# An MLP up projection in seven products (Strassen) instead of eight, with the down projection as a stage of its own

## The chip, the cores and the metric

The kernel runs on one core of a Trainium2 chip. The metric is device time in microseconds (us) of one execution. The time before is the median of three runs: 3092.51 us (3089.76 to 3093.38).

## The reference, cut to what matters

One decoder layer over 2048 positions of width 1024: a mixer of two attention groups with an output projection, and then a gated MLP. The change concerns the MLP and the place where it begins:

```python
x = x + _rmsnorm(mix, attn_post_norm[l])
h = _rmsnorm(x, ffn_pre_norm[l])                       # 2048 x 1024
u = _causal_depthwise_conv(h @ w_up[l], conv_w[l], conv_b[l])   # w_up: 1024 x 5632, three taps
gate, val = jnp.split(u, 2, axis=-1)                   # 2816 columns each
y = (jax.nn.gelu(gate, approximate=True) * val) @ w_down[l]     # w_down: 2816 x 1024
x = x + _rmsnorm(y, ffn_post_norm[l])
```

## The kernel before

All data are float32. Every operand of a product is split into a part `hi`, copied to the type fp32r, and the rest `lo`, and each product is three matmuls: hi·hi, hi·lo, lo·hi. The helper `split` (L455) makes the two parts: `hi` is a copy on ACT or DVE, `lo` a subtraction on POOL or DVE.

The order of the whole program is made when it is built. Every piece of work is an `op` with an engine, a guessed duration, the ops it depends on, its buffers and a due time (`plan.now` minus `lead`). `Plan.run` (L180) plays a list schedule: at each instant each engine takes the ready op with the earliest due time whose buffers are free, and the instruction is written into that engine's stream. An op with `.alt` goes to whichever of two engines is free first. In the guesses a POOL op and a DVE op never hold each other up (`c_pool(512)` is 1223 ns, `c_dvs(512)` 664 ns), and all transfers, which go through SP's one queue, share 250 GB/s; SP hands out no more than 3 us of transfers ahead. On the chip each engine runs its stream in that fixed order and waits on semaphores. Buffers come from tags with a fixed number of copies, handed out in the order in which the program asked for them.

The output projection runs in blocks of 128 positions (`wo_block`, 16 of them): a load of the mixer's output, 48 matmuls, the post norm, the residual row block `x1` (stored to `x1d`, L1125), the pre norm of the MLP, eight transposes, and a store of the transposed rows to `h2d` (L1148).

The MLP goes over four token tiles of 512 positions (`t`), one after the other. For each tile there are 44 up jobs (22 feature tiles `m` of 128 columns, gate and value, `up`): 8 k-blocks of 128 times three matmuls 128x128 by 512, into one PSUM bank; then DVE and ACT do the convolution's three taps (L1238 to L1240), GELU (L1243) and the product (L1248), and ACT and POOL split the result into `gt` (L1249, L1250), which stays in SBUF. Then come 22 down jobs (`down`, L1311): eight accumulators of 128x512, 24 matmuls for each `m`. Weights are loaded and split for every token tile (`weights`, four jobs ahead). The memory of the MLP's inputs and weights lies where the attention's buffers were (`ffn_left`), so up jobs of tile 0 start before the last output-projection blocks are done; the rest (`ffn_right`) opens when those blocks are.

## Time and profile before

| | |
|---|---|
| median of three runs | 3092.51 us |
| profiled execution | 3094.23 us, of which the span from the first to the last instruction is 3092.5 us |
| TensorE (PE) busy | 2984.5 us, 97% of the span |
| VectorE (DVE) busy | 2252.0 us, 73% |
| ScalarE (ACT), GpSimd (POOL) busy | 1442.9 us (47%), 951.6 us (31%) |
| transfers | 437.11 MB, mean 141 GB/s |
| mean granted TensorE clock | 0.992 |

PE overlaps successive matmuls, so its busy time counts a matmul longer than the distance between two of them. DMA share is the mean busy share of the 16 DMA engines.

### The profile page before, as it was taken

Reading aid. Unit: us, or ns where it says so; the run is one execution under the profiler, and the core shown is the slowest. Engines: PE = TensorE matmul, PEld = TensorE weight load, DVE = VectorE, ACT = ScalarE, POOL = GpSimd, SP = SyncE. Lnnn points to the kernel's source line nnn. Section 1 sums busy time; section 2 is a strip of 40 time slices with the busy share of each in tenths; the row PEclk is TensorE's granted clock in tenths of the full one; section 3 lists DMA queues with packets and bytes.
Section 4 is the critical chain, followed back from the end, with each engine's and each line's share of the span. In section 5 each row is a group of like instructions: output and inputs, shape, how many; then the busy total and the mean of one; then the engine's idle time right before and its main releaser. Section 6 shows DMA issues by size and latency. Waiting matters only on the chain. (4 is left out here: it accounts for less than half of the span.)

```text
span 3092.5 us, 48117 instructions
## 1 busy us (share of the span) xinstructions
PE 2984.5 (97%) x17352; PEld 2610.4 (84%) x17352; DVE 2252.0 (73%) x4327; ACT 1442.9 (47%) x2913; POOL 951.6 (31%) x1047
## 2 busy tenths in 40 slices
PE   7999999999999999889999999999999999999998
PEld 7899999999888888868877888888888888888887
DVE  4658878897999999998754864387744776277742
ACT  4434545555777767666643433233322433233321
POOL 1001002002766777675411211033301332023310
PEclk9999999999999999999999999999999999999999
DMA  8776656655634366533363333443344333343332
GB/s 264 246 209 186 185 151 201 171 156 159 188 122 130 95 194 185 151 100 112 110 214 126 102 100 116 121 134 96 96 129 143 96 99 106 119 141 101 96 123 82
DMA packets 392146, 437.11 MB, mean 141 GB/s; under 512 B 20096, under 2 KB 328164, under 8 KB 381668
## 3 DMA queue, kind: packets, MB, share of 16 engines
q1 hardware_dynamic: 391908, 434.05, 46.7%
q8 instruction: 136, 2.23, 0.3%
q14 instruction: 102, 0.84, 0.1%
HBM read 333.30 MB, written 100.67 MB: 140 GB/s over the span
## 5 line engine op out<-in xcount | busy, mean ns | idle before, releaser
L1226 PE MATMUL pu<-fh,fhi 128*128 128x512 f32 x2816 | 869.0, 390 | 0.2 <-ACT fu L1234 0.2
L1226 PEld LDWEIGHTS pu<-fh,fhi 128*128 128x128 f32 x2816 | 529.4, 188 | 110.5 <-ACT fu L1234 0.6
L461 DVE TENSOR_TENSOR flo<-fraw,fhi 128x1024 fp32r<-128x1024 f32 x186 | 233.0, 1254 | 488.6 <-ACT fhi L458 488.5
L1226 PE MATMUL pu<-fh,flo 128*128 128x512 f32 x1408 | 549.2, 390 | 0.0
L982 POOL TENSOR_TENSOR ring_w<-ring_w,ring_a 128x512 f32<-128x512 f32 (+2 forms) x320 | 387.9, 1224 | 220.3 <-DVE ring_a L977 121.1
L605 PE MATMUL g<-hT,big 128*128 128x256 f32 x3072 | 447.8, 288 | 7.3 <-DVE st L638 4.3
L458 ACT CAST fhi<-fraw 128x1024 fp32r<-128x1024 f32 x253 | 265.5, 1051 | 397.4 <-PE py L1311 218.6
L1311 PE MATMUL py<-fhi,gt 128*128 128x512 f32 x1408 | 435.9, 390 | 0.0
L605 PEld LDWEIGHTS g<-hT,big 128*128 128x128 f32 x3072 | 405.4, 192 | 19.8 <-DVE st L638 4.4
L977 DVE TENSOR_TENSOR_SCAN ring_a<-ring_a 128x513 f32<-128x513 f32 (+2 forms) x320 | 412.8, 1316 | 6.1 <-ACT ring_a L969 6.1
L702 PE MATMUL z<-k,q 128*128 128x512 f32 (+3 forms) x1280 | 362.5, 376 | 10.4 <-ACT ring_a L969 7.0
L466 ACT CAST thi<-t 128x512 fp32r<-128x512 f32 (+2 forms) x472 | 221.6, 492 | 210.1 <-PE t L720 179.3
L1311 PEld LDWEIGHTS py<-fhi,gt 128*128 128x128 f32 x1408 | 264.5, 188 | 60.0
L1226 PEld LDWEIGHTS pu<-fh,flo 128*128 128x128 f32 x1408 | 264.7, 188 | 54.9
L734 DVE TENSOR_TENSOR tlo<-t,thi 128x512 fp32r<-128x512 f32 (+2 forms) x528 | 281.6, 556 | 34.6 <-ACT thi L466 28.4
L459 POOL TENSOR_TENSOR flo<-fraw,fhi 128x1024 fp32r<-128x1024 f32 x78 | 195.8, 2510 | 338.9 <-DVE fhi L457 171.2
L1311 PE MATMUL py<-flo,gt 128*128 128x512 f32 x704 | 277.8, 395 | 0.0
L720 PE MATMUL t<-ident,ring_w 128*128 128x128 f32 x1632 | 253.2, 276 | 22.4 <-DVE tlo L734 18.5
L1250 POOL TENSOR_TENSOR gt<-fy,gt 128x512 fp32r<-128x512 f32 x88 | 118.4, 1347 | 493.9 <-ACT gt L1249 483.0
L1239 DVE SCALAR_TENSOR_TENSOR fy<-fu,cw,fy 128x512 f32<-128x512 f32 x176 | 239.6, 1361 | 6.2
L384 POOL TENSOR_TENSOR sm<-sm,neghalf 128x2 f32<-128x2 f32 (+1 forms) x72 | 76.8, 1067 | 536.5 <-DVE sm L382 534.7
L602 PE MATMUL g<-big,hT 128*128 128x256 f32 x1536 | 227.4, 288 | 6.3 <-DVE st L624 1.5
(158 smaller groups left out, 4697.4 us busy)
## 6 DMA issues: line engine op xcount, KB each, us to landing
fraw<-in_w_up_dram SPq DMA_DIRECT2D x176, 512.0 KB, 3.8
hT<-hd SPq DMA_DIRECT2D x64, 1024.0 KB, 7.0
fraw<-in_w_down_dram SPq DMA_DIRECT2D x88, 512.0 KB, 3.8
q<-qd SPq DMA_DIRECT2D x128, 256.0 KB, 4.3
hd<-hT SPq DMA_DIRECT2D x16, 1024.0 KB, 5.4
qd<-st SPq DMA_DIRECT2D x128, 128.0 KB, 2.6
kd<-st SPq DMA_DIRECT2D x128, 128.0 KB, 2.6
vd<-st SPq DMA_DIRECT2D x64, 256.0 KB, 5.2
```

The lines of the kernel that those rows point to most:

```text
L458: "ACT", c_act(n) + 42, lambda: nc.scalar.copy(hi(), raw()))
L461: "DVE", c_dvs(n), lambda: nc.vector.tensor_tensor(lo(), raw(), f32(hi()), ALU.subtract))
L602: nc.tensor.matmul(ps.t[:, cs], hk[:, b, c * P:(c + 1) * P], wv[:, a, k, :], start=first, stop=last)
L605: nc.tensor.matmul(ps.t[:, cs], wv[:, a, k, c * P:(c + 1) * P], hk[:, b, :], start=first, stop=last)
L702: nc.tensor.matmul(ps.t[:, 0:w], q.t[:, m, l, jj * P:(jj + 1) * P], kt.t[:, m, 0:w], start=(l == 0), stop=(l == 1 and not masked))
L720: nc.tensor.transpose(ps.t[:, cc * P:(cc + 1) * P], rows[jj].t[:, (k + kk) * P:(k + kk + 1) * P], ident)
L734: ol = op("DVE", c_dvp(n), lambda sl=sl: nc.vector.tensor_tensor(lo.t[:, sl], ps.t[:, sl], f32(hi.t[:, sl]), ALU.subtract), (oh,), (ps, hi ...
L977: nc.vector.tensor_tensor_scan(gr, gr, gr, 1.0 if cb is None else cb[0].t[:, 0:1], ALU.mult, ALU.bypass)
L982: rdeps.append(op("POOL", c_pool(w), lambda be=be, gm=gm, w=w: nc.gpsimd.tensor_tensor(be.t, be.t, gm.t[:, 1:w + 1], ALU.mult), (o1, o2), ...
L1226: nc.tensor.matmul(ps.t, w3(w)[:, k, :], h.t[:, a, k, :], start=(k == 0 and i == 0), stop=(k == KD - 1 and i == 2))
L1239: nc.vector.scalar_tensor_tensor(y.t, u.t[:, 1:TT + 1], cw[:, 1, f:f + 1], y.t, ALU.mult, ALU.add)
L1311: nc.tensor.matmul(ps.t, gt.t[:, a, j * P:(j + 1) * P], wt.t[:, ms], start=(m == 0 and i == 0), stop=(m == NFT - 1 and i == 2))
```

## The change

The up projection of gate and value over two token tiles of 512 is seen as a product of two 2x2 block matrices: rows gate and value by two halves of K (weights), two halves of K by two token tiles (inputs). The Winograd form of Strassen's scheme needs seven block products instead of eight, with sums of blocks on both sides and sums of the products after. `S` is a pair of token tiles, so there are 44 up steps (`S`, `m`) with 7 times 12 matmuls each.

`combos` builds the seven input blocks, split, one k-block at a time, from `h2q` and stores them in DRAM (`bd`); `load_b` loads the seven of a pair (2 MB each), five into memory that opens with `ffn_left` and two into `ffn_right`. `up_weights` loads four weight quarters, makes four sums on DVE and seven splits. `up` runs the seven products, copies the first from PSUM, makes seven sums of PSUM and SBUF tiles on DVE, and convolves both tiles at once (1024 wide; the first tap on ACT). The gated product is split and stored to `gtd`. The down projection is a loop of its own: for each (`t`, `m`) it loads and splits 2 x 256 KB of weights and loads 512 KB of `gtd`. The order is up of pair 0, down of tile 0, up of pair 1, down of tiles 1 to 3. `ffn_left` opens at the attention's end as before, but everything that an up step needs besides the input blocks now lies in `ffn_right`.

```diff
-    h2d = [dram.tile([P, KD, P], F32, name=f"h2d{i}") for i in range(NB)]
+    h2q = [dram.tile([P, KD, TT], F32, name=f"h2q{t}") for t in range(NTT)]
+    bd = [dram.tile([P, 2 * 4 * TT], F32, name=f"bd{i}") for i in range(14)]
+    gtd = [dram.tile([NFT, P, 2 * TT], F32, name=f"gtd{t}") for t in range(NTT)]
...
-                h2d[b].rearrange("p k n -> p (k n)"), h2.t), ops, (h2,), 0, 1 << 19, "h2store")
+                h2q[b // 4][:, :, b % 4 * P:(b % 4 + 1) * P], h2.t.rearrange("p (k n) -> p k n", k=KD)), ops, (h2,), 0, 1 << 19, "h2store")
...
-    for name, n in (("fraw", 2), ("fhi", 4), ("flo", 4), ("fh", 1), ("fu", 2), ("fy0", 2), ("fy1", 2), ("yh", 4),
-                    ("x1", 1), ("o1", 2), ("junk", 1), ("gt", NFT), ("pu", 4), ("py", 4), ("fs", 16)):
-        T[name] = Tag(n, fifo=name != "fs", bank=name in ("pu", "py"))
...
+    PROD = ("11", "21", "t2", "t1", "t3", "22", "t4")
+    for name, n in (("hb", 4), ("gt", 3), ("B", 5), ("B2", 2), ("Wc", 7), ("wr", 5), ("sS", 2), ("sa", 4), ("fu", 2),
+                    ("y", 2), ("fs", 16), ("pf", 8)):
+        T[name] = Tag(n, fifo=name != "fs", bank=name == "pf")
...
+        fill_tags(hp, {"hb": ([P, 512], F32), "gt": ([P, 2, TT], F32R), "B": ([P, 2, 4, TT], F32R)})
...
+        fill_tags(gp, {"B2": ([P, 2, 4, TT], F32R), "Wc": ([P, 2, 512], F32R), "wr": ([P, 512], F32),
+                       "sS": ([P, 512], F32), "sa": ([P, 512], F32), "fu": ([P, 2 * TT + 2], F32),
+                       "y": ([P, 2 * TT], F32), "fs": ([P, 4], F32)})
+        fill_tags(pool(rpsum, "pf8", "right", PSUM), {"pf": ([P, 512], F32)})
...
+    def combos(S, k):
+
+        def get(half, t):
+            b = buf("hb")
+            tt = 2 * S + t
+            return b, load(lambda: b.t, h2q[tt][:, half * 4 + k, :], 1 << 18, (b,),
+                           [h2store[4 * tt + j] for j in range(4)], what="hbload")
+
+        def sub(x, y):
+            (a, ao), (b, bo) = x, y
+            d = buf("hb")
+            return d, op("DVE", c_dvs(512), lambda: nc.vector.tensor_tensor(d.t, a.t, b.t, ALU.subtract), (ao, bo),
+                         (d, a, b), what="hsub")
+
+        def emit(name, x):
+            a, ao = x
+            g = buf("gt")
+            o = split(lambda: a.t, lambda: g.t[:, 0, :], lambda: g.t[:, 1, :], 512, (ao,), (a, g), 0.0)
+            bstore[S, name].append(op(SPE, 0, lambda: nc.sync.dma_start(
+                bd[S * NC7 + PROD.index(name)].rearrange("p (a k n) -> p a k n", a=2, k=4)[:, :, k, :], f32(g.t)), o,
+                (g,), 0, 1 << 19, "bstore"))
+
+        b11, b12 = get(0, 0), get(0, 1)
+        t1 = sub(b12, b11)
+        emit("11", b11)
+        b22 = get(1, 1)
+        t3 = sub(b22, b12)
+        emit("t1", t1)
+        t2 = sub(b22, t1)
+        emit("22", b22)
+        emit("t3", t3)
+        b21 = get(1, 0)
+        t4 = sub(b21, t2)
+        emit("t2", t2)
+        emit("21", b21)
+        emit("t4", t4)
...
+    def load_b(S):
+        for i, name in enumerate(PROD):
+            b = buf("B" if i < 5 else "B2")
+            assert len(bstore[S, name]) == 4
+            btile[S, i] = b, load(lambda b=b: f32(b.t).rearrange("p a k n -> p (a k n)"), bd[S * NC7 + i], 1 << 21, (b,),
+                                  bstore[S, name], lead=10e3, what="bload")
...
+    def up_weights(S, m):
+        raw = {}
+        for i, c in ((0, 0), (0, 1), (1, 0), (1, 1)):
+            r = buf("wr")
+            f = i * NFT + m
+            raw[i, c] = r, load(lambda r=r: r.t.rearrange("p (k n) -> p k n", k=4),
+                                up_src[:, c * 4:(c + 1) * 4, f * P:(f + 1) * P], 1 << 18, (r,), lead=0.0, what="wup")
+
+        def comb(d, x, y, alu, deps=()):
+            (a, ao), (b, bo) = x, y
+            return d, op("DVE", c_dvs(512), lambda: nc.vector.tensor_tensor(d.t, a.t, b.t, alu), (ao, bo, *deps),
+                         (d, a, b), what="wsub")
+
+        res = []
+
+        def emit(x):
+            a, ao = x
+            w = buf("Wc")
+            res.append((w, split(lambda: a.t, lambda: w.t[:, 0, :], lambda: w.t[:, 1, :], 512, (ao,), (a, w), 0.0)))
+
+        emit(raw[0, 0])
+        emit(raw[0, 1])
+        s1 = comb(buf("sS"), raw[1, 0], raw[1, 1], ALU.add)
+        s2 = comb(buf("sS"), s1, raw[0, 0], ALU.subtract)
+        emit(s2)
+        emit(s1)
+        emit(comb(buf("sS"), raw[0, 0], raw[1, 0], ALU.subtract))
+        emit(comb(s2[0], raw[0, 1], s2, ALU.subtract, res[2][1]))
+        emit(raw[1, 1])
+        return res
...
+    def up(S, m):
+        ws = made.pop(("U", S, m))
+
+        def prod(i):
+            ps, (w, wd), (b, bl) = buf("pf"), ws[i], btile[S, i]
+            o = None
+            for k2 in range(2):
                 def go(k2=k2):
+                    wv = w.t.rearrange("p a (k n) -> p a k n", k=4)
                     for k in (2 * k2, 2 * k2 + 1):
-                        for i, (w, a) in enumerate(((hi, 0), (hi, 1), (lo, 0))):
-                            nc.tensor.matmul(ps.t, w3(w)[:, k, :], h.t[:, a, k, :],
-                                             start=(k == 0 and i == 0), stop=(k == KD - 1 and i == 2))
-                last = op("PE", 6 * c_mm(512), go, [*ls, *wd, last] if last else [*ls, *wd], (hi, lo, h, ps), what="up")
-                plan.now += 6 * c_mm(512)
+                        for n, (x, y) in enumerate(((0, 0), (0, 1), (1, 0))):
+                            nc.tensor.matmul(ps.t, wv[:, x, k, :], b.t[:, y, k, :], start=k == 0 and n == 0,
+                                             stop=k == 3 and n == 2)
+                o = op("PE", 6 * c_m2(512), go, [*wd, bl] + ([o] if o else []), (ps, w, b), what="up")
+            plan.now += 12 * c_m2(512)
+            return ps, o
...
+        p1 = prod(0)
+        a = buf("sa")
+        a = a, copy(lambda a=a: a.t, lambda: p1[0].t, 512, (p1[1],), (p1[0], a))
+        c11 = add(ua(fg), fg, a, prod(1))
+        b = part(a, prod(2))
+        p5 = prod(3)
+        d = part(b, p5)
+        c = part(b, prod(4))
+        c22 = add(ub(fv), fv, c, p5)
+        c12 = add(ub(fg), fg, d, prod(5))
+        c21 = add(ua(fv), fv, c, prod(6))
...
+            o = op("ACT", c_act(2 * TT) + 95, lambda: nc.scalar.activation(
+                y.t, u.t[:, 0:2 * TT], AF.Identity, scale=sc(0), bias=sc(3)), (o0, *deps, *mem["cw"]), (u, y),
+                what="conv")
+            for i in (1, 2):
+                o = op("DVE", c_dvs(2 * TT), lambda i=i: nc.vector.scalar_tensor_tensor(
+                    y.t, u.t[:, i:2 * TT + i], sc(i), y.t, ALU.mult, ALU.add), (o,), (u, y), what="conv")
...
+        for t in range(2):
+            sl = slice(t * TT, (t + 1) * TT)
+            g = buf("gt")
+            o1 = op("DVE", c_dvs(512), lambda sl=sl: nc.vector.tensor_tensor(yv.t[:, sl], yg.t[:, sl], yv.t[:, sl],
+                                                                           ALU.mult), (o, og), (yg, yv))
+            os_ = split(lambda sl=sl: yv.t[:, sl], lambda g=g: g.t[:, 0, :], lambda g=g: g.t[:, 1, :], 512, (o1,),
+                        (yv, g), 0.0)
+            gstore[2 * S + t, m] = op(SPE, 0, lambda g=g, t=t: nc.sync.dma_start(
+                gtd[2 * S + t][m], f32(g.t).rearrange("p a n -> p (a n)")), os_, (g,), 0, 1 << 19, "gstore")
...
+    def down_weights(t, m):
+        ws = []
+        for h in range(2):
+            r, w = buf("wr"), buf("Wc")
+            o = load(lambda r=r: r.t, w_down[0, m * P:(m + 1) * P, h * 512:(h + 1) * 512], 1 << 18, (r,), lead=0.0,
+                     what="wdn")
+            ws.append((w, split(lambda r=r: r.t, lambda w=w: w.t[:, 0, :], lambda w=w: w.t[:, 1, :], 512, (o,), (r, w),
+                                0.0)))
+        g = buf("gt")
+        gl = load(lambda: f32(g.t).rearrange("p a n -> p (a n)"), gtd[t][m], 1 << 19, (g,), (gstore[t, m],), lead=0.0,
+                  what="gload")
+        return ws, g, gl
...
+        ss, o, x1 = T["fs"].buf(), buf("y"), buf("fu")
...
+        items = [("U", 0, m) for m in range(NFT)] + [("D", 0, m) for m in range(NFT)] + [
+            ("U", 1, m) for m in range(NFT)] + [("D", t, m) for t in range(1, NTT) for m in range(NFT)]
+        ready = 0
+
+        def prepare(n):
+            nonlocal ready
+            while ready <= min(n, len(items) - 1):
+                kind, a, m = it = items[ready]
+                made[it] = up_weights(a, m) if kind == "U" else down_weights(a, m)
+                ready += 1
+        for n, (kind, a, m) in enumerate(items):
...
+            prepare(n + (1 if kind == "U" and items[min(n + 1, len(items) - 1)][0] == "U" else 3))
+            if kind == "U":
+                up(a, m)
+                if a == 0 and m in (3, 7, 11, 15):
+                    combos(1, (3, 7, 11, 15).index(m))
+            elif m < NFT - 2:
+                down(a, m, range(4))
+                if a == 0 and m == 0:
+                    load_b(1)
+            elif m == NFT - 1:
                 for j in range(4):
-                    for i in range(4):
-                        down(W[n - 1 + i // 2], t, NFT - 4 + i, v, (j,))
+                    for mm in (NFT - 2, NFT - 1):
+                        down(a, mm, (j,))
...
+    op(None, 0, ffn_left, users("k", "v", "q", "thi", "tlo", "mo", "ot", "os", "sq", "mix", "sm", "z", "o", "w", "a"))
     for b in range(8, NB):
         run(wo_block(b))
+        if b < 12:
+            combos(0, b - 8)
+    load_b(0)
```

The parts left out: pools' names, the loaders and helper calls inside the functions shown, the halo copies (as before, two values for each feature tile), GELU and product (as before, 1024 wide and in two halves of 512), `finish` (as the old `half`, 1024 wide, one store of 512 KB), and the removed bodies, which stand in the listing above.

## Rows read from the trace of the kernel before

**Rows 1.** Chain that ended last, in time: start, us, engine, line, matmuls.

```profile
1680.78 12.29 PE pu L1226 x54
...
2002.97 239.36 PE pu L1226 x1056
2242.33 120.86 PE py L1311 x528
```

**Rows 2.** Window, up jobs of tile 1: length, busy PE, PEld, DVE, ACT, POOL (instructions), PEclk, DMA share, GB/s.

```profile
2003.00:2242.00 239.00, 239.00 (x1056) 198.05 (x1055) 181.54 (x266) 90.19 (x131) 83.69 (x45) 1.00 0.38 113
```

**Rows 3.** Groups by line, PE, 1583 to 1682: count, busy us, mean ns.

```profile
L1226 PE MATMUL pu<-fh,fhi 128*128 128x512 f32 x120 | 38.0, 398 | 0.0
```

**Rows 4.** Groups by line, DVE and POOL, up jobs of tile 1 (2003 to 2242).

```profile
L1239 DVE SCALAR_TENSOR_TENSOR fy<-fu,cw,fy 128x512 f32<-128x512 f32 x42 | 65.9, 1568 | 1.5
L1240 DVE SCALAR_TENSOR_TENSOR fy<-fu,cw,fy 128x512 f32<-128x512 f32 x42 | 31.6, 752 | 1.5
L1238 DVE TENSOR_SCALAR fy<-fu,cw 128x512 f32<-128x512 f32 x42 | 31.3, 745 | 0.0
L461 DVE TENSOR_TENSOR flo<-fraw,fhi 128x1024 fp32r<-128x1024 f32 x22 | 28.1, 1276 | 53.9 <-ACT fhi L458 53.9
L1282 DVE TENSOR_TENSOR o<-py,gfpost 128x512 f32<-128x512 f32 x2 | 1.4, 685 | 0.0
L459 POOL TENSOR_TENSOR flo<-fraw,fhi 128x1024 fp32r<-128x1024 f32 x22 | 55.1, 2507 | 47.7 <-ACT fhi L458 44.1 <-DVE fs L1284 3.6
L1250 POOL TENSOR_TENSOR gt<-fy,gt 128x512 fp32r<-128x512 f32 x21 | 27.2, 1298 | 109.7 <-ACT gt L1249 104.2 <-PE pu L1226 5.5
```

**Rows 5.** Instructions in time, DVE and POOL, one conv: start, us.

```profile
2101.64 0.54 DVE L1238 TENSOR_SCALAR fy<-fu,cw 128x512 f32<-128x512 f32 x1
2102.22 2.77 DVE L1239 SCALAR_TENSOR_TENSOR fy<-fu,cw,fy 128x512 f32<-128x512 f32 x1
2105.02 0.75 DVE L1240 SCALAR_TENSOR_TENSOR fy<-fu,cw,fy 128x512 f32<-128x512 f32 x1
2105.69 0.16 DVE L1235 COPY halo<-fu 128x2 f32<-128x2 f32 x1
...
2101.90 2.54 POOL L459 TENSOR_TENSOR flo<-fraw,fhi 128x1024 fp32r<-128x1024 f32 x1 [2.08 <-ACT fhi L458]
```

**Rows 6.** Instructions in time: DVE reading PSUM (`t`) beside POOL, in the attention.

```profile
899.31 1.26 DVE L734 TENSOR_TENSOR tlo<-t,thi 128x512 fp32r<-128x512 f32 x2
...
898.38 1.89 POOL L982 TENSOR_TENSOR ring_w<-ring_w,ring_a 128x512 f32<-128x512 f32 x1 [1.22 <-DVE ring_a L977]
```

**Rows 7.** Groups by line, ACT, 1680 to the end.

```profile
L458 ACT CAST fhi<-fraw 128x1024 fp32r<-128x1024 f32 x244 | 256.1, 1051 | 390.2 <-PE py L1311 218.6 <-PE pu L1226 116.6 <-DMA fraw<-in_w_down_dram 51.9
L1234 ACT COPY fu<-pu 128x512 f32<-128x512 f32 x169 | 98.1, 580 | 9.7 <-DVE fy L1240 5.2 <-DVE halo L1235 4.5
```

**Rows 8.** Windows with the DMA engines full: the last two columns.

```profile
120.00:130.00 10.00, 10.00 (x88) 10.00 (x87) 8.83 (x31) 8.09 (x22) 1.39 (x2) 1.00 0.96 327
510.00:520.00 10.00, 10.00 (x80) 9.64 (x79) 9.37 (x32) 3.98 (x8) 0.00 (x0) 1.00 1.02 291
```

**Rows 9.** DMA issues in time, SP queue, output projection: `x1` of blocks 8, 10, 15.

```profile
1548.47 0.46 SPq L377 DMA_DIRECT2D fraw<-h2d  x1
1550.82 0.33 SPq L1125 DMA_DIRECT2D x1d<-r  x1
...
1583.55 0.33 SPq L1125 DMA_DIRECT2D x1d<-r  x1
...
1685.30 0.33 SPq L1125 DMA_DIRECT2D x1d<-r  x1
```

**Rows 10.** DMA issues by kind: count, KB each, median us to landing.

```profile
fraw<-in_w_up_dram SPq DMA_DIRECT2D x176, 512.0 KB, 3.8
```

**Rows 11.** Instructions in time: the last matmul and the last DVE instruction.

```profile
3083.22 0.39 PE L1311 MATMUL py<-fhi,gt 128*128 128x512 f32 x1
...
3088.72 0.75 DVE L1294 SCALAR_TENSOR_TENSOR o<-o,fs,fh 128x512 f32<-128x512 f32 x1
```

More of the change, by code (lines that the diff above doesn't have):

```diff
@@ new lines, in prod, with add, part @@
+            plan.now += 12 * c_m2(512)
+            return ps, o
+        def add(dst, dbuf, x, p):
+            (a, ao), (ps, o) = x, p
+            return op("DVE", c_dvp(512), lambda: nc.vector.tensor_tensor(dst(), ps.t, a.t, ALU.add), (ao, o),
+                      (ps, a, dbuf), what="uadd")
+        def part(x, p):
+            d = buf("sa")
+            return d, add(lambda: d.t, d, x, p)
+        fg, fv = buf("fu"), buf("fu")
+        ua = lambda f: (lambda: f.t[:, 2:TT + 2])
+        ub = lambda f: (lambda: f.t[:, TT + 2:2 * TT + 2])
@@ L1320, in ffn_all @@
-        AHEAD = 4
-        for j in range(4):
-            load_h2(0, j, ())
-        for n in range(AHEAD):
-            weights(n)
-        for n, (kind, t, m, v) in enumerate(jobs):
-            if n + AHEAD < len(jobs):
-                weights(n + AHEAD)
-            if kind == "up":
-                up(n, t, m, v)
-            elif m < NFT - 4:
-                w = W.pop(n)
-                down(w, t, m, v, range(4))
-                down(w, t, m + 1, v, range(4))
-                if v == 0 and t + 1 < NTT and m in (4, 8, 12, 16):
-                    load_h2(t + 1, m // 4 - 1, (lasts[t, 0, 3],))
-            elif m == NFT - 2:
+            if S == 0:
+                halod[f] = op("DVE", 70, lambda: nc.vector.tensor_copy(halo[:, f, :], u.t[:, 2 * TT:2 * TT + 2]),
+                              (o0, *deps), (u,))
@@ new lines, in layer_kernel, with down, go @@
+    dn = {}
+    def down(t, m, js):
+        ws, g, gl = made["D", t, m]
+        for j in js:
+            for h, (w, wd) in enumerate(ws):
+                if m == 0:
+                    dn[t, j, h] = buf("pf"), None
+                ps, prev = dn[t, j, h]
+                def go(j=j, ps=ps, w=w):
+                    for i, (a, b) in enumerate(((0, 0), (0, 1), (1, 0))):
+                        nc.tensor.matmul(ps.t, g.t[:, a, j * P:(j + 1) * P], w.t[:, b, :],
+                                         start=(m == 0 and i == 0), stop=(m == NFT - 1 and i == 2))
+                dn[t, j, h] = ps, op("PE", 3 * c_m2(512), go, [gl, *wd] + ([prev] if prev else []), (ps, g, w),
+                                     what="dn")
+                plan.now += 3 * c_m2(512)
+            if m == NFT - 1:
+                finish(t, j)
```

168 lines of the change are left out of this document (38 added, 130 removed).

## The prediction

> **What bounds the kernel now.** I read the chain of work that ended last first, because it tells which engine sets the end. Its long last links are TensorE alone: the 1056 matmuls of a token tile's up jobs take 239.36 us and the 528 of its down jobs 120.86 us, one behind the other [rows 1]. That is 0.2267 us for an up matmul and 0.2289 us for a down matmul. Then I read the window of one tile's up jobs: PE full, DVE busy 181.5 of 239 us, POOL 83.7 [rows 2]. So a matmul less is worth its 0.2267 us, as long as nobody makes TensorE wait. The groups of instructions [rows 3, 4, 7], the instructions in time [rows 5, 6], full DMA windows [rows 8] and the SP queue [rows 9, 10] are for what the change puts beside it.
>
> **The terms.** The sum starts from the profiled execution, 3094.2 us (its span and 1.7 us around it); the median of the runs is 1.7 us below.
>
> *Matmuls.* 44 steps of 84 instead of 96: 528 x 0.2267 = 119.7 us less. The 2112 down matmuls stay, and a step of the up projection is now 84 x 0.2267 = 19.0 us, one of the down projection 24 x 0.2289 = 5.5 us. Minus 119.7.
>
> *The beginning of the MLP.* Today up jobs of tile 0 fill the gaps of the last output-projection blocks: 120 hi matmuls and half as many with lo weights between 1583 and 1682 [rows 3], 180 or 40.8 us that are done when, from about 1682 on, up matmuls have PE to themselves [rows 1]. After the change no up matmul can run before `ffn_right` opens, which waits for the last block. So the 40.8 us come back, and the first product starts late. How late: the memory of `ffn_left` is open from 1548 [rows 9]. From there on these transfers stand before the first step: blocks 9 to 15 (7 x 2.1 MB), `combos(0)` (28 stores of 0.52 MB, 16 loads of 0.26 MB), seven tiles of 2.1 MB, the gain and the first weights (1.5 MB); together 49.8 MB. With full DMA engines windows moved 327 and 291 GB/s [rows 8]: 152 to 171 us, middle 162, so 1710. The weights are behind the last two tiles in the queue (these are due 10 us earlier), and behind them come some 2 us to the landing (3.8 for a load of 1.6 us of data [rows 10]) and a split (0.6 + 1.3 [rows 4, 7]): first product at 1714, 32 us after 1682. Term 40.8 + 32 = plus 73. From below: the blocks' own chain. `x1` of block 8 leaves at 1550.8, of block 10 at 1583.6 [rows 9], 16.4 us a block; block 15 would be at 1665, and some 8 us of norm and transposes, a store, 5.7 MB and the split make 1691: plus 50. From above: 20.4 us a block as from 10 to 15 [rows 9], and one tile in the way: 1733, plus 92.
>
> *The tiles of pair 1.* They take the memory that the last step of pair 0 frees. Down steps 0 to 2 are prepared at the beginning of that step, but step 3's loads are due at the beginning of down step 0, and `load_b(1)` is due 4.6 us before that. So in the queue: 3.1 MB of steps 0 to 2, 14.7 MB of tiles, two stores of the gated product, 1.0 MB for step 3. By 327 GB/s the 19.9 MB take 61 us, and 2 us to land; TensorE has work for 19.0 + 3 x 5.5 = 35.5 us. Plus 27 of stall (22 if the two stores stand behind, 35 by 291 GB/s). Down steps later take 1.05 MB per 5.5 us, 191 GB/s, which fits, so nothing is won back. The Trainium skill (HBM Reference, Specifications) says that a core that streams alone measures about 425 GB/s; no window of this trace shows more than 327 (small packets among them). By that rate this stall would be 14 us and the sum 13 us less, an estimate from that page.
>
> *DVE and POOL in an up step.* What DVE gets, in distances between starts (0.67 for two SBUF operands of 512 [rows 5], 0.63 from PSUM [rows 6], some 1.2 for 1024 [rows 4], less the overlap of two): four weight sums 2.7, four taps of 1024 4.8, two products 1.3, seven sums from PSUM 4.4, halo copies 0.3. Of the splits' subtractions the schedule gave DVE 22 and POOL 22 in tile 1, where either could have them [rows 4]; of nine I give DVE 3.5 (2.3 us) and POOL 5.5 (7.1 us by 1.30 [rows 4]). Most `hi` parts go to ACT, which has 2 x 1.05 (first taps), about 1.05 (GELU), 0.6 and 8 x 0.6 = 8.6 us [rows 7] of 19, so they cost nothing; one on DVE 0.35. DVE's sum is 16.2 of 19.0 us. By these durations TensorE still sets the pace, and the term is zero.
>
> But the two engines do not run side by side. In [rows 5] the second tap, two SBUF operands, starts 0.3 us after a POOL subtraction and lasts 2.77 us instead of 0.75: it ends 0.55 us after POOL's end. Over the tile the second tap means 1568 ns against 752 for the same work at the third, and the first tap 745 against 540: 34 + 9 = 43 us that DVE stood, 51% of POOL's 83.7 us [rows 2, 4, 5]. An operation that reads PSUM was not held: two of 0.63 us pass beside a POOL operation [rows 6]. The Trainium skill (SBUF — State Buffer, Who interferes with whom) gives the rule: DVE with two SBUF inputs and GpSimd reading SBUF shut each other out for a whole instruction; the 2.77 us agree. By durations alone the sum would be 3089, with the lock it is that of the next lines.
>
> In the new step DVE has little idle time beside which POOL could pass (before, 57 of 239 us [rows 2]), only the 4.4 us of PSUM sums. So the share of POOL's time that stops DVE lies between 0.51 and, with the PSUM sums as the only cover, 0.78; I take 0.63. A step is 16.2 + 0.63 x 7.1 = 20.6 us, 1.6 over TensorE: 35 us in each pair. Pair 0 also has `combos(1)`: 16 sums and 28 subtractions, 10.7 + 9.4 on DVE, 14 x 1.3 x 0.63 = 11.5 of standing: 32 us more. Of the 102 us I take off 12, since the weights are split one step ahead and the backlog at a pair's end falls into down steps, where DVE is free. Plus 90; from below 28 (share 0.51, all lead used), from above 170 (6.5 subtractions on POOL, 0.78).
>
> *Changes of stage.* The three `gt` copies go to down steps 0 to 2 before the last up step's two, so in pair 1 step 3's load waits for step 2's end: 4 us. In `finish` a third row block waits for the first one's store (two copies of its buffers), and its PSUM banks with it: some 3 us at two tile changes, 2 us elsewhere. Plus 12 (3 to 20). At the end, 10.6 us today from the last matmul [rows 11] to the end of the execution, the same wait adds 3 (1 to 6). The other additions (2.1 MB stores of `h2q`, `gtd`) lie in up steps whose DMA share is 0.38 [rows 2] and stay hidden.
>
> Sum: 3094.2 - 119.7 + 73 + 27 + 90 + 12 + 3 = 3179.5, against the median's base 3178.
>
> **Rivals.** *TensorE keeps the pace in the up steps* (the other side). The place is the up step. POOL's subtractions pass beside sums from PSUM and DVE's remaining gaps; it decides at 2.9 us of standing per step (19.0 - 16.2), a share of 0.41. For it speaks that in tile 1 PE stood nowhere while DVE was busy 76% [rows 1, 2]; against it that half of POOL's time stopped DVE even then. Time: 3179.5 - 90 = 3089, between 3050 and 3128 with the beginning's bounds (50 to 92) and the others': faster where the beginning comes out under 71. Chance 0.24: 0.14 faster, 0.04 equal, 0.06 slower.
>
> *The last block is caught behind the tiles.* Its residual row is due 5 us before the stage's end, the tiles 10 us; if five tiles (10.5 MB) are in the queue before it, `ffn_right` opens 32 us later: 3210. For it: the order of due times; against it, that at 16.4 us a block the row is asked for at about 1660, by when `combos` has hardly let the first tiles go. Chance 0.12.
>
> *The tiles of pair 1 are hidden*, if step 3's loads find a free copy early and pass the tiles: 3151. Against it stands the due time. Chance 0.06.
>
> The forecast itself, DVE and POOL over TensorE in the up steps, has 0.58, with 3105 to 3255 as its own range. About 0.2% (6 us) is what a measurement can tell. Faster: 0.14 of the first rival and 0.04 of the forecast's low end, 0.18; equal 0.06; slower 0.76. The range 3070 to 3262 leaves out the fast half of the first rival and the top of the forecast.
>
> **What would show it.** In the profile after: 3696 up matmuls; a gap of PE of some 30 us or more before the first one, at about 1714; one of some 27 us after the third down step of tile 0; in the up steps PE waiting for `Wc` subtractions, DVE busy 95% or more, taps of 1024 that mean well over 1.3 us, POOL's subtractions over 1.3, pair 0 slower than pair 1 by some 1.4 us a step. Wrong it would be above all if a step of pair 1 takes 19.0 us, or if the first product starts before 1690.

## The result and the profile after

The changed kernel takes 3192.72 us (median of 4 runs, 3190.27 to 3195.74) against 3091.14 us for the kernel before (4 runs): ratio 1.0329, 95% interval [1.0311, 1.0347]. It is slower by 3.3%, in spite of 528 matmuls less. The profiled execution took 3194.84 us, its span 3193.1.

The page of the changed kernel, engine totals and the two costliest groups (their last field is the time that TensorE stood before them):

```profile
PE 2935.2 (92%) x16824; PEld 2531.8 (79%) x16824; DVE 2457.2 (77%) x4479; ACT 1470.9 (46%) x3014; POOL 1122.0 (35%) x1154
...
L1277 PE MATMUL pf<-B,Wc 128*128 128x512 f32 x3696 | 877.2, 399 | 64.0 <-POOL Wc L461 22.9
...
L1364 PE MATMUL pf<-Wc,gt 128*128 128x512 f32 x2112 | 502.1, 400 | 35.7 <-DMA gt<-gtd 33.2
```

Some 100 us of standing lie in the MLP, where before the long links of the chain had none [rows 1]. Windows by stage tell where (the same columns as in [rows 2]): the last output-projection blocks, the wait for the first product, up steps of pair 0, down steps of tile 0, up steps of pair 1, down steps of tiles 1 to 3.

```profile
1547.00:1687.00 140.00, 90.83 (x346) 69.91 (x345) 63.96 (x107) 49.06 (x128) 20.69 (x25) 0.80 0.87 305
1687.00:1725.90 38.90, 8.13 (x37) 6.11 (x35) 5.42 (x13) 7.98 (x25) 1.10 (x2) 0.66 0.59 204
1725.90:2204.80 478.90, 447.38 (x1849) 356.46 (x1850) 460.69 (x587) 188.37 (x270) 248.21 (x141) 0.96 0.41 137
2204.60:2358.90 154.30, 128.85 (x530) 103.15 (x529) 51.90 (x76) 37.53 (x65) 7.45 (x7) 0.90 0.72 259
2358.70:2799.10 440.40, 429.85 (x1849) 346.22 (x1847) 419.21 (x516) 175.27 (x248) 213.62 (x123) 1.00 0.32 106
2801.60:3182.60 381.00, 373.22 (x1584) 299.74 (x1584) 130.27 (x189) 96.27 (x175) 22.80 (x22) 0.99 0.63 209
```

The reader is to see three things: DMA at 305 GB/s ahead of the first product; DVE busy 96% and 95% of the two up stages, with TensorE short of full; and the first down stage 33 us longer than the 120.86 of [rows 1]. TensorE in time, at these three places (the bracket is the idle time before the instruction and what ended it):

```profile
1701.97 1.97 PE L1141 MATMUL t<-ident,r 128*128 128x128 f32 x8 [6.63 <-DVE r L1132]
1725.89 4.47 PE L1277 MATMUL pf<-B,Wc 128*128 128x512 f32 x10 [21.95 <-ACT Wc L460]
...
2219.08 14.09 PE L1364 MATMUL pf<-Wc,gt 128*128 128x512 f32 x48 [7.29 <-DMA gt<-gtd]
2250.16 10.19 PE L1364 MATMUL pf<-Wc,gt 128*128 128x512 f32 x32 [16.99 <-DMA gt<-gtd]
...
2573.30 39.21 PE L1277 MATMUL pf<-B,Wc 128*128 128x512 f32 x168 [1.32 <-POOL Wc L461]
2614.35 26.01 PE L1277 MATMUL pf<-B,Wc 128*128 128x512 f32 x111 [1.84 <-POOL Wc L461]
```

The last two rows show the pace of pair 1 late in the stage: 168 matmuls, two steps, and then 1.84 us of waiting for a GpSimd subtraction. Pair 1 cut at the place where these waits begin:

```profile
2358.70:2572.00 213.30, 213.28 (x921) 172.49 (x919) 203.19 (x253) 85.13 (x122) 102.17 (x60) 1.00 0.33 108
2572.00:2799.00 227.00, 216.47 (x928) 173.73 (x928) 215.92 (x264) 90.14 (x127) 111.42 (x64) 1.00 0.31 105
```

Eleven steps (921 matmuls) run without a gap at 213.3 / 10.96 = 19.5 us each; the next eleven take 227.0 / 11.05 = 20.5. The lock that sets these 20.5 is seen in DVE and POOL in time: at 2576 a DVE subtraction starts 0.2 us after one of POOL and takes 1.64 us, and at 2579.97 the same operation, with POOL idle, 0.69.

```profile
2576.36 1.64 DVE L463 TENSOR_TENSOR Wc<-sS,Wc 128x512 fp32r<-128x512 f32 x1
...
2579.97 0.69 DVE L463 TENSOR_TENSOR Wc<-sS,Wc 128x512 fp32r<-128x512 f32 x1 [0.16 <-ACT Wc L460]
...
2576.16 1.29 POOL L461 TENSOR_TENSOR Wc<-sS,Wc 128x512 fp32r<-128x512 f32 x1
```

### The profile page after: what moved, and what is told of

It reads as the page before. It is cut to its first block, busy times and chain, and to the rows that moved or that the text cites. A ratio compares the mean times of both kernels' runs of the same rounds, so it can differ in the third digit from the quotient of the medians.

```text
span 3193.1 us, 48827 instructions
## 1 busy us (share of the span) xinstructions
PE 2935.2 (92%) x16824; PEld 2531.8 (79%) x16824; DVE 2457.2 (77%) x4479; ACT 1470.9 (46%) x3014; POOL 1122.0 (35%) x1154
## 5 line engine op out<-in xcount | busy, mean ns | idle before, releaser
L1277 PE MATMUL pf<-B,Wc 128*128 128x512 f32 x3696 | 877.2, 399 | 64.0 <-POOL Wc L461 22.9
L1277 PEld LDWEIGHTS pf<-B,Wc 128*128 128x128 f32 x3696 | 702.5, 191 | 238.5 <-POOL Wc L461 28.6
L1364 PE MATMUL pf<-Wc,gt 128*128 128x512 f32 x2112 | 502.1, 400 | 35.7 <-DMA gt<-gtd 33.2
L1364 PEld LDWEIGHTS pf<-Wc,gt 128*128 128x128 f32 x2112 | 402.8, 191 | 134.8 <-ACT Wc L460 17.4
L461 POOL TENSOR_TENSOR Wc<-wr,Wc 128x512 fp32r<-128x512 f32 x137 | 259.7, 1903 | 318.3 <-ACT Wc L460 153.5
L460 ACT CAST Wc<-wr 128x512 fp32r<-128x512 f32 x260 | 159.5, 617 | 378.1 <-PE pf L1364 296.5
L1320 DVE SCALAR_TENSOR_TENSOR y<-fu,cw,y 128x1024 f32<-128x1024 f32 x176 | 279.9, 1601 | 25.0 <-ACT y L1316 23.7
L722 PEld LDWEIGHTS t<-ident,ring_w 128*128 128x128 f32 x1632 | 188.9, 141 | 39.7 <-issue 14.5
L704 PEld LDWEIGHTS z<-k,q 128*128 128x128 f32 x1280 | 199.5, 190 | 23.3 <-ACT ring_a L971 12.4
L604 PEld LDWEIGHTS g<-big,hT 128*128 128x128 f32 x1536 | 205.7, 193 | 13.2 <-DVE st L626 2.4
```

The lines of the kernel that those rows point to most:

```text
L460: "ACT", c_act(n) + 42, lambda: nc.scalar.copy(hi(), raw()))
L461: o2 = op("POOL", c_pool(n), lambda: nc.gpsimd.tensor_tensor(lo(), raw(), f32(hi()), ALU.subtract), (o1,), bufs, lead, what="split").alt(" ...
L604: nc.tensor.matmul(ps.t[:, cs], hk[:, b, c * P:(c + 1) * P], wv[:, a, k, :], start=first, stop=last)
L704: nc.tensor.matmul(ps.t[:, 0:w], q.t[:, m, l, jj * P:(jj + 1) * P], kt.t[:, m, 0:w], start=(l == 0), stop=(l == 1 and not masked))
L722: nc.tensor.transpose(ps.t[:, cc * P:(cc + 1) * P], rows[jj].t[:, (k + kk) * P:(k + kk + 1) * P], ident)
L1277: nc.tensor.matmul(ps.t, wv[:, x, k, :], b.t[:, y, k, :], start=k == 0 and n == 0, stop=k == 3 and n == 2)
```

## The experiments

The theory was the prediction's: transfers set the beginning, the tiles of pair 1 stall the first down stage, and the lock between DVE and GpSimd sets the up steps. The rivals were that DVE's own work is too long, that the transfers are hidden behind the blocks' chain, and that a gain at one place is handed back at the next. Unless said otherwise, a variant ran once, beside a run of the kernel before of 3090 to 3093 us; gains are counted from the changed kernel's 3192.72.

**GpSimd writes instead of subtracting.** In up steps and `combos` GpSimd writes zeros twice where it would subtract, so the low halves that it makes are missing from the products.

```diff
+    def split_w(raw, hi, lo, n, deps, bufs, lead):
+
+        def twice():
+            nc.gpsimd.memset(f32(lo()), 0.0)
+            nc.gpsimd.memset(f32(lo()), 0.0)
...
+        o2 = op("POOL", c_pool(n), twice, (o1,), bufs, lead, what="split").alt(
```

> In the up steps and in the input sums, POOL's way of a split writes zeros twice over the lo part instead of reading two operands and subtracting; DVE's way stays, and so does the written order of all work. Left out by it: the lo parts that POOL made are zero. Lock theory (a POOL instruction that reads SBUF stops every DVE instruction with two SBUF operands): the second and third taps fall from 1.60 us to about 1.25, the up stages from 478.9 and 440.4 us to 419 to 428 each, the whole to about 3120 us. Rival, DVE's own work (its 16 us of sums and taps per step and the written order hold TensorE up, whoever else runs): both stages stay within 10 us, the whole above 3170.

3115.09 us, 78 less. Up steps of both pairs and the taps of pair 1 in this run:

```profile
1725.00:2155.00 430.00, 430.00 (x1856) 348.48 (x1855) 372.70 (x597) 198.20 (x273) 147.74 (x276) 1.00 0.47 159
2298.60:2726.70 428.10, 428.10 (x1850) 347.06 (x1849) 354.32 (x526) 186.59 (x254) 132.71 (x241) 1.00 0.34 115
...
L1331 DVE SCALAR_TENSOR_TENSOR y<-fu,cw,y 128x1024 f32<-128x1024 f32 x84 | 106.8, 1281 | 17.1 <-ACT y L1327 16.3
```

GpSimd is still busy 132.7 us of pair 1, but it reads nothing, and DVE hardly stands: taps take 1281 ns against 1613, and TensorE has no gap. The lock is real and costs up to 478.9 - 430 = 49 us in pair 0 and 12 us in pair 1. Up to, because GpSimd's turn is shorter too: two writes take 1.1 us, an undisturbed subtraction 1.29.

**Halo copies on ScalarE.** In the changed kernel these tiny copies had become expensive on DVE; the run below without GpSimd's subtractions has them at 161 ns (groups by line, pair 1 of the changed kernel; the first tap group and GpSimd's subtractions beside them):

```profile
L1320 DVE SCALAR_TENSOR_TENSOR y<-fu,cw,y 128x1024 f32<-128x1024 f32 x84 | 134.7, 1613 | 16.6 <-ACT y L1316 15.8
L461 POOL TENSOR_TENSOR Wc<-wr,Wc 128x512 fp32r<-128x512 f32 x66 | 127.4, 1938 | 156.4 <-DVE Wc L459 77.8 <-ACT Wc L460 66.9 <-PE pf L1277 11.6
L461 POOL TENSOR_TENSOR Wc<-sS,Wc 128x512 fp32r<-128x512 f32 x35 | 55.7, 1593 | 39.5 <-ACT Wc L460 38.9 <-DVE Wc L459 0.6
L463 DVE TENSOR_TENSOR Wc<-sS,Wc 128x512 fp32r<-128x512 f32 x52 | 45.2, 869 | 3.2 <-ACT Wc L460 3.1
L1311 DVE COPY fu<-halo 128x2 f32<-128x2 f32 x43 | 31.2, 746 | 0.0
L461 POOL TENSOR_TENSOR gt<-y,gt 128x512 fp32r<-128x512 f32 x20 | 30.8, 1539 | 29.6 <-ACT gt L460 29.6
L463 DVE TENSOR_TENSOR gt<-y,gt 128x512 fp32r<-128x512 f32 x20 | 24.7, 1234 | 0.0
L1245 DVE TENSOR_TENSOR sS<-sS,wr 128x512 f32<-128x512 f32 x21 | 19.0, 903 | 0.0
```

```diff
-            o0 = op("DVE", 70, lambda: nc.vector.tensor_copy(u.t[:, 0:2], halo[:, f, :]),
+            o0 = op("ACT", 200, lambda: nc.scalar.copy(u.t[:, 0:2], halo[:, f, :]),
...
-                halod[f] = op("DVE", 70, ...
+                halod[f] = op("ACT", 200, ...
```

> The halo copies (two values for each feature tile, on DVE, four per step in pair 0 and two in pair 1) go to ACT; everything is computed. Lock theory: these copies are held by POOL like the others (746 ns mean in pair 1, 580 and 455 in pair 0, for two columns), so DVE gets back some 31 us in pair 1 and 42 in pair 0; the up stages become 420 to 430 and 440 to 455 us, the whole 3140 to 3160. Rival, DVE's own work: the copies are two columns wide, 84 and 42 of them at 0.07 us free nothing; the whole within 6 us of 3193.

3192.45 us: no gain, the time that the rival had named; pair 1 went from 440.4 to 438.6. The product of the two convolutions, 706 ns before, and a weight sum, 679 before, now stand (window and groups by line, pair 1 of this run):

```profile
2358.50:2797.10 438.60, 429.73 (x1849) 346.24 (x1847) 404.12 (x484) 177.38 (x282) 214.44 (x122) 1.00 0.32 107
...
L1331 DVE TENSOR_TENSOR y<-y,y 128x512 f32<-128x512 f32 x41 | 31.9, 818 | 0.0
L1245 DVE TENSOR_TENSOR sS<-wr,sS 128x512 f32<-128x512 f32 x21 | 21.4, 1017 | 11.8 <-POOL Wc L461 11.8
```

So the standing moved to the neighbours in part only. DVE was busy 15 us less (404.1 instead of 419.2), and still TensorE won 2: DVE now waits 11.8 us for GpSimd's subtractions. In these steps the two engines also wait for each other in turn, so time given back to DVE alone shortens nothing. To take away the instruction that stands frees almost nothing; the one that makes it stand has to go.

**All low halves of an up step on DVE.** High halves on ScalarE, the nine subtractions on DVE, none on GpSimd.

```diff
+    def split_v(raw, hi, lo, n, deps, bufs, lead):
+        o1 = op("ACT", ..., lambda: nc.scalar.copy(hi(), raw()), ...)
+        o2 = op("DVE", c_dvs(n), lambda: nc.vector.tensor_tensor(lo(), raw(), f32(hi()), ALU.subtract), (o1,), ...)
```

> In the up steps all hi parts go to ACT and all nine subtractions to DVE; POOL gets none there (combos and down steps keep both ways). Everything is computed. Lock theory: DVE's own sum is then some 19.7 us per step without standing, against 20.5 measured: pair 1's stage 428 to 437 instead of 440.4, pair 0's 455 to 470 instead of 478.9, the whole 10 to 35 us less, although the busier engine got more work. Rival, DVE's own work sets the pace: with 3.5 subtractions more per step (2.3 us) both stages grow by 30 to 50 us each, the whole is 60 to 100 us more.

3136.32 us, 56 less where 10 to 35 were expected, with more work for DVE. Pair 0 took 441.1 us (455 to 470 expected). Pair 1: window, and groups of DVE.

```profile
2318.60:2746.70 428.10, 428.10 (x1849) 346.74 (x1847) 399.45 (x608) 197.29 (x285) 7.07 (x7) 1.00 0.34 111
...
L1327 DVE SCALAR_TENSOR_TENSOR y<-fu,cw,y 128x1024 f32<-128x1024 f32 x84 | 104.6, 1300 | 3.2 <-ACT y L1323 2.8
L469 DVE TENSOR_TENSOR Wc<-sS,Wc 128x512 fp32r<-128x512 f32 x86 | 56.3, 685 | 2.4 <-ACT Wc L468 2.3
...
L1318 DVE COPY fu<-halo 128x2 f32<-128x2 f32 x42 | 5.0, 161 | 0.0
```

DVE does 22 x 9 subtractions in 399 us, less than the 419 it was busy when GpSimd had 121 of them (the 24 high halves that it copied then, 10 us, are on ScalarE now). This decides against "DVE's own work": that alone fits, and TensorE sets the pace.

**Tiles of pair 0 written by the splits.** Five of the seven go straight to their tiles; 21 MB less through DRAM.

```diff
+            if S == 0 and name not in ("22", "t4"):
+                b, os_ = btile[S, i]
+                os_.extend(split(lambda: a.t, lambda: b.t[:, 0, k, :], lambda: b.t[:, 1, k, :], 512, ...))
+                return
```

> The splits of pair 0's input blocks write five of the seven tiles in SBUF themselves; only the two tiles whose memory opens last go through DRAM. 21 MB fewer of stores and loads stand before the first product; everything is computed. If transfers set the beginning, as the prediction has it, the first product moves from 1725.9 to between 1690 and 1705 and the whole falls by 20 to 35 us. Rival, the blocks' own chain of waits sets it: the first product stays above 1718, the whole within 8 us of 3193.

3151.12 us, 42 less; the first product is at 1680.20, even earlier than expected:

```profile
1656.25 1.94 PE L1141 MATMUL t<-ident,r 128*128 128x128 f32 x8 [8.77 <-DVE fu L1318]
1680.20 9.97 PE L1284 MATMUL pf<-B,Wc 128*128 128x512 f32 x34 [22.01 <-ACT Wc L460]
```

The last block's transposes move from 1702 to 1656, and the wait behind them stays 22 us. So it was the transfers that held the blocks back.

**The first step's weights at the front of the queue** (they are due 40 us earlier), and **the tiles of pair 1 one by one** (a tile every third down step instead of all at the first, and due no earlier than its step).

```diff
-                                ..., (r,), lead=0.0, what="wup")
+                                ..., (r,), lead=40e3 if (S, m) == (0, 0) else 0.0, what="wup")
...
-                if a == 0 and m == 0:
-                    load_b(1)
+                if a == 0 and m % 3 == 0:
+                    load_b(1, (m // 3,))
```

> The four weight loads of the first up step are due 40 us earlier, so that in the queue they stand ahead of the last two input tiles and the gain; everything is computed. By the prediction's step (weights behind 4.7 MB in the queue) the first product moves from 1725.9 to about 1713 and the whole falls by 9 to 14 us. Rival: the wait only moves into the first step, where the sixth and seventh products then wait for their tiles; the whole within 4 us of 3193.

> The seven input tiles of pair 1 are due one by one, at down steps 0, 3, 6 and so on to 18, instead of all at the beginning of the stage; everything is computed. If the stall of that stage is the tiles' place in the queue ahead of step 3's loads, the down stage of tile 0 falls from 154.3 to 122 to 132 us and the whole by 20 to 30 us. Rival, the stage's transfers themselves (38 MB) are too many: the stage stays above 140 us, the whole within 12 us.

3188.91 and 3193.27 us: each did what it was to do at its place, and neither is worth more than 4 us. With the weights first, the first product came at 1712.06 instead of 1725.89 (9.6 us behind the last transposes instead of 22), but TensorE stands at the next down stage, here and for another 20.6 us ahead of the fourth step (its instructions in time):

```profile
2203.07 18.69 PE L1364 MATMUL pf<-Wc,gt 128*128 128x512 f32 x72 [9.79 <-DMA gt<-gtd]
```

With the tiles spread, the first down stage took 140.2 us instead of 154.3, and pair 1 449.3 instead of 440.4; 1.4 us more stand between them:

```profile
2205.20:2345.40 140.20, 128.68 (x529) 102.64 (x527) 46.12 (x66) 34.16 (x60) 8.10 (x6) 0.94 0.75 270
2346.80:2796.10 449.30, 432.42 (x1848) 347.20 (x1848) 424.76 (x523) 176.34 (x248) 216.51 (x124) 1.00 0.33 109
```

So most of what was won at these two places was handed back later. My reading, which no run tested by itself, is that while DVE sets the up stages a stall of TensorE before them is time in which DVE catches up. It fits the spread tiles, where TensorE has to wait from pair 1's first matmuls on. With the weights first the up stage took 481 us instead of 479, and the larger part was lost in the down stage's waits for `gt`, 30.4 us instead of 24.3. And it is no general rule: the tiles written directly kept the 46 us of an earlier first product nearly whole, with DVE as busy as before.

**`combos(1)` in the first down stage**, straight to the tiles: `combos(1, m // 4)` at down steps 0, 4, 8, 12, no loads of tiles.

> Pair 1's input blocks are made in the down stage of tile 0 and written into their tiles directly, instead of in pair 0's up steps through DRAM; everything is computed. By the prediction's terms pair 0's up stage loses its 32 us of sums and subtractions (478.9 to about 445, as pair 1), and the down stage of tile 0 its tiles in the queue (154.3 to 126 to 138): the whole falls by 45 to 65 us. Rival: pair 0 is slower for another reason (its clock of 0.96, its first steps); then its stage stays above 465 and only the down stage gains, 15 to 25 us in all.

3152.31 us, 40 less where 45 to 65 were expected. Pair 0 fell from 478.9 to 445.0, the amount that was expected; the down stage with the work in it only from 154.3 to 146.5, less than expected (it still waits 11 us for a `gt`):

```profile
1720.60:2165.60 445.00, 436.86 (x1848) 351.38 (x1848) 424.79 (x555) 177.31 (x248) 213.05 (x122) 0.98 0.31 103
```

**All that helped, together**, with the copy of the first product on ScalarE as well, which no run tried alone; and the same with the last step's gated product in two `Wc` tiles, so that all `gt` tiles are free for the down steps.

```diff
-            g = buf("gt")
+            g = buf("gt" if m < NFT - 1 else "Wc")
```

> All four edits that helped, together: both pairs' tiles written straight from the splits (pair 1's during the first down stage; the last two of pair 0 still go through DRAM), the first step's weights at the front of the queue, all low halves of the up weights on DVE instead of GpSimd, and the copy of each step's first product on ScalarE. If the three causes (transfers at the beginning, the tiles behind the down loads, the lock between GpSimd and DVE) are separate places of the timeline, their gains add: first product 1655 to 1680, the up stages 425 to 440 each, the first down stage 140 to 148, the rest as in the change; 3055 to 3085 in all, which is faster than the kernel before. If each gain is given back at the next wait, as the two queue edits showed: 3090 to 3120.

> As the run with everything together, and in the last step of each pair the split gated products go to two weight tiles instead of two of the three tiles that the down steps read, so that those three are free for the down steps' loads. If the wait after the third down step is for these three tiles, the gaps of about 11 and 5 us at the head of the first down stage and of 3 and 5 us after pair 1 fall below 3 each, 10 to 20 us less than the run with everything. If the wait is for the transfers themselves, no change.

Together: 3059.07 us (4 runs), ratio to the kernel before 0.9899, 95% [0.9882, 0.9916]. With the gated tiles: 3058.21 us (4 runs), 0.9894 [0.9879, 0.9909]. Both beat the kernel before, by 1%. By themselves four of the edits won 42, 40, 56 and 4 us, 142 in all, and with the fifth 134 came together (3192.7 to 3059.1). The total nearly adds, the places do not. In pair 0's up stage `combos(1)` moved away and the low halves on DVE had won 34 and 38 us alone and win 43 together, since both remove the same wait. Of the 14 us of the weights first, handed back alone, some 10 now count: the first product comes 56 us earlier, with the direct tiles alone 46. That this is because DVE no longer sets the pace fits, but no run shows it apart. The stages with everything together:

```profile
1669.80:2105.50 435.70, 432.12 (x1848) 349.01 (x1848) 402.84 (x640) 200.15 (x287) 11.41 (x8) 0.99 0.35 117
2111.80:2242.30 130.50, 127.57 (x529) 102.85 (x530) 71.82 (x98) 46.12 (x81) 21.90 (x17) 0.96 0.66 221
2242.10:2670.20 428.10, 428.10 (x1849) 346.73 (x1847) 397.18 (x604) 197.46 (x286) 8.74 (x7) 1.00 0.34 111
2672.80:3047.80 375.00, 372.18 (x1584) 298.34 (x1584) 124.27 (x184) 95.41 (x173) 18.91 (x20) 1.00 0.62 209
```

TensorE waits 6.3 us ahead of the first down stage, and that stage takes 130.5, better than expected. So the gated tiles had little left to win: that stage fell to 126.7 and the last three to 373.3, some 5 us in all, which the medians don't tell from nothing; the expected 10 to 20 was missed.

**Where the operands lie.** The up matmuls never reached the 226.7 ns of before: pair 1 without any gap takes 428.1 / 1848 = 231.7 ns each. Three runs went after it: 1056 bytes of unused memory ahead of the input tiles; the tiles of products 1 and 2 on the right instead of 6 and 7; and, on the best version, weights on the left with the tiles of products 1 to 3 (the third edit is given in short).

```diff
+        hp.tile([P, 264], F32, name="pad")
...
-            b = buf("B" if i < 5 else "B2")
+            b = buf("B" if i >= 2 else "B2")
...
-("B", 5), ("B2", 2)        "Wc" in ffn_right        "B" if i < 5
+("B", 3), ("B2", 4)        "Wc" in ffn_left         "B" if i < 3
```

> A tile of 1056 bytes per partition that nobody uses is put ahead of the input tiles in memory, so that the five tiles of the first products lie 1056 bytes higher; nothing else changes. In the run before, matmuls of products 2 to 5 follow each other in 233.7 ns, those of the seventh product in 226.7 ns, and the down matmuls are slower too. If the place of a tile in SBUF relative to the weights makes the difference, these distances change and the up stages lose up to 9 us each. Rival: the distance has to do with the order of products or with which engine writes at the time; then it stays at 233.7.

> Only the place of the input tiles is changed: products 1 and 2 read tiles in the memory on the right (beside the weights), products 3 to 7 tiles in the memory on the left; before it was 1 to 5 left, 6 and 7 right. If the place of the moving tile sets the distance between matmuls, products 1 and 2 fall to 227 to 229 ns and 6 and 7 rise to 233 to 235. If it is what else happens during a product (the order of the step), products 2 to 5 stay at 233 to 235 and 6 and 7 at 227 to 229. Whole time 3185 to 3200 either way.

> On the run with everything and free gate tiles: the split weights now lie in the memory on the left, with the input tiles of products 1 to 3 only; products 4 to 7 read tiles on the right. Of pair 0, four tiles instead of two go through DRAM (6 MB more of transfers at the beginning, so the whole may be 10 to 25 us longer). If the matmul is slow when its two operands lie on different sides, products 1 to 3 follow each other at 227 to 230 ns and 4 to 7 at 233 to 235 in the second pair. If the left side is the slow place for the input tile wherever the weights are, 1 to 3 stay at 233 to 235 and 4 to 7 fall to 227 to 230.

3193.55, 3186.28 and 3050.14 us (the 10 to 25 us more that were expected of the third did not come). The pad changed next to nothing. Matmuls of one product in time; 13 of them with the last one's 0.39 us in 3.19 us are 233 ns apart, in 3.11 us 227. The changed kernel, product 3 (tile left, weights right) and product 7 (both right, x14):

```profile
2539.18 3.19 PE L1277 MATMUL pf<-B,Wc 128*128 128x512 f32 x13
...
2550.32 3.34 PE L1277 MATMUL pf<-B,Wc 128*128 128x512 f32 x14
```

With other tiles on the right, product 2 (both right) and product 6 (tile left):

```profile
2528.48 3.14 PE L1277 MATMUL pf<-B,Wc 128*128 128x512 f32 x13
...
2539.60 3.19 PE L1277 MATMUL pf<-B,Wc 128*128 128x512 f32 x13
```

With weights on the left, product 3 (both left) and product 6 (tile right):

```profile
2423.45 3.11 PE L1291 MATMUL pf<-B,Wc 128*128 128x512 f32 x13
...
2431.75 3.19 PE L1291 MATMUL pf<-B,Wc 128*128 128x512 f32 x13
```

In all three the slow ones, 233 ns, are those whose two operands lie on different sides, and neither the product's number nor the left side decides. Averaged by product over pair 1 of the same three traces (products ahead of which TensorE waits left out), the distances are 226.7 to 229.5 ns for operands on one side and 231.8 to 233.7 for operands on two. The place decides, then, but it is no rule of the sides alone: in the kernel before the down matmuls stream weights from the left against `gt` on the right, and follow each other every 228.9 ns [rows 1]. The down steps of the last run, whose weights and `gt` now both lie on the left, took 365.0 us for tiles 1 to 3 instead of 373.3:

```profile
2672.60:3037.60 365.00, 360.61 (x1584) 296.84 (x1584) 125.00 (x186) 96.44 (x174) 17.14 (x18) 1.00 0.64 215
```

## Why the prediction was right, and where its terms were not

The sum was 3179.5 for the profiled execution; it came out at 3194.84. The mechanism of the forecast held in the main, several of its sizes did not, and two of these errors, the matmuls' distance and the lock, partly cancel; that is luck.

*Matmuls*, minus 119.7: the count is right (3696). But the step "84 x 0.2267" was not: at 231.7 ns, 1848 matmuls take 428.1 instead of 418.9, so the two pairs together lose 18 us that no term had. The cause is the place of the operands, above.

*Beginning*, plus 73: measured 1725.9 - 1682 + 40.8 = 85, inside its bounds (50 to 92). The bytes were right: 140.0 us at 305 GB/s and 38.9 at 204 are 50.6 MB, counted 49.8. The step that failed is the rate to the end: the last 39 us, the last block's chain and its 22 us of wait, don't fill the DMA engines (0.59 of them busy). The gap just before the first product was 22 us, not the 30 or more named as a sign. That transfers and not the blocks' own chain set it, the runs with direct tiles showed.

*Tiles of pair 1*, plus 27: the waits for `gt` are 7.3 us after the first down step and 17.0 after the third, 24.3 together; the forecast had all of it after the third. The size came out, the way to it less so. The issues of the SP queue, and windows (columns as in [rows 2]) of down steps 1 and 2, of the wait, and of what follows it:

```profile
2210.40 2.80 SPq L379 DMA_DIRECT2D B<-bd  x5
...
2233.20 0.33 SPq L379 DMA_DIRECT2D gt<-gtd  x1
```

```profile
2219.00:2233.20 14.20, 14.09 (x48) 10.97 (x48) 2.15 (x4) 1.24 (x2) 0.00 (x0) 0.79 1.02 434
2233.20:2250.10 16.90, 0.00 (x0) 0.00 (x0) 1.36 (x2) 1.24 (x2) 0.00 (x0) 0.56 1.00 412
2250.16:2254.00 3.84, 3.84 (x9) 3.07 (x10) 1.36 (x2) 1.83 (x3) 0.00 (x0) 0.50 1.04 388
```

Five of the seven tiles leave at 2210 to 2213 and one at 2208.7, after the up stage's end and not during its last step. Step 3's `gt` is asked for at 2233.20, in the moment in which step 2 ends and frees a copy, and lands 17 us later behind the tiles. The transfers were faster than the 327 GB/s of the estimate, 434 and 412; the 425 that the Trainium skill states for a core that streams alone (HBM Reference, Specifications) agree with these two. (The trace before had more than 327 as well: 346 from 810 to 820.) So a later start of the tiles and a faster transfer cancelled, by luck. The stage as a whole is 33 longer: 8 of these are TensorE's own time, 128.85 busy instead of 120.86, most of it by the granted clock. After 17 us without a matmul its granted clock was 0.50, the lower level of 1.2 GHz: nine matmuls in 3.84 us.

*DVE and GpSimd*, plus 90: the up stages took 478.9 + 440.4, 81.5 over 2 x 418.9. Of that the matmuls' distance is 18 and the lock and `combos(1)` together 63 (with GpSimd's reads gone, 49 + 12 went). So the lock was over-sized. GpSimd's part came out as assumed (121 subtractions in 22 steps, 5.5 each). The share of its time that stops DVE did not: against the rows without GpSimd's reads DVE stood (1613 - 1300) x 84 + (746 - 161) x 43 + (869 - 685) x 52 + (1234 - 686) x 20 + (903 - 686) x 21 ns = 77 us in pair 1; of 121 x 1.29 = 156 us that is 0.49, not 0.63. A third of it fell on the halo copies, which the prediction's share, read from the taps, did not include. A step in the steady state still took 20.5 us, where 20.6 was forecast, since DVE also waits (227.0 - 215.92) / 11.05 = 1.0 us a step. This agreement is partly luck. The forecast took a step to be DVE's sum and its standing; with the halo copies on ScalarE DVE had 15 us less in pair 1, and a step still took 20.4 us. The turns in which DVE and GpSimd wait for each other are part of the step, and the forecast had no term for them. The lead is the other size: it covered eleven steps, 11 x (20.5 - 19.5) = 11 us, in pair 1 alone. The rule that the Trainium skill gives (SBUF — State Buffer, Who interferes with whom), that DVE with two SBUF inputs contends with a GpSimd instruction that reads SBUF and not with one that only writes it, agrees with the taps: 1613 ns beside reads, 1281 beside writes. The Trainium skill also says there that copies, when their operands meet its conditions, can use both of DVE's port pairs and contend; 746 against 161 ns agree.

*Changes of stage*, plus 12: the last three down stages took 381.0 instead of 3 x 120.86 = 362.6, 18.4 more, of which 7.8 are gaps (381.0 - 373.2) and 10.6 matmuls, and 2.5 lie ahead of them; 20.9 is just over the 20 that the forecast allowed. *Tail*, plus 3: 10.5 us behind the last matmul in the span, 1.6 more than before [rows 11].

By measured terms: 3094.2 - 119.7 + 84.7 + 33.4 + 81.5 + 20.9 + 1.6 = 3196.6.

*Rivals.* "TensorE keeps the pace" needed a share of standing under 0.41; 0.49 stood. It is what the kernel does once GpSimd subtracts nothing. "The last block caught behind the tiles" did not happen: the `x1` rows of blocks 8 to 15 left between 1548.8 and 1699.1, 21.5 us apart on average (more than the 20.4 of the forecast's upper bound), and the last 16 behind the one before. "Pair-1 tiles hidden" did not happen either.

Of the 10.6 us of slower matmuls in the last down stages, some 4 lie in the first 72, right behind waits: 24 in 7.38 us and 48 in 12.95, at a granted clock of 0.77 and 0.87. The other 1512 are 233 ns apart, with `gt` on the left and the weights on the right; the run with both on the left took 8.3 us less for the three stages. Open stays what it is about the operands' places that makes them slow. The two sides as such it can hardly be, by the down matmuls of the kernel before; the distance between the addresses no run varied by itself by more than 1056 bytes. Eight products in the new structure, which would price the sums of Strassen's scheme alone, weren't tried.

## What to carry to other kernels

A saving on the bound engine is worth only what the next engine lets through: add up that engine's step with the time that a neighbour makes it stand, and give the neighbour no work that locks it, even if the busy engine must do more itself (56 us won by moving work from a half-idle GpSimd to a 95% busy DVE). Remove the instruction that causes the standing, not the one that shows it. And while a second engine has a backlog, a stall of TensorE that is shortened by itself can come back later in the program: 14 us at two places left 4 and nothing, 46 us at a third stayed. So read the next stages before you call a stall won, and expect two edits that remove the same wait not to add.

## What the runs showed of the hardware that wasn't expected

- In the new up projection a matmul of 512 columns with a new weight tile follows the one before after 227 to 229 ns when input and weights lie in the same of the two memory pools, after 232 to 234 when they lie in different ones, in three arrangements; 1056 bytes of shift change next to nothing. That is about 18 us in the up projection. The down matmuls of the kernel before, 228.9 ns with operands in different pools, show that the pool alone does not decide.
- A DVE copy of 128x2 elements took 746 ns on average beside GpSimd's subtractions, 161 ns without them.
